# A decoder layer in float32 on one core: the last job keeps its split weights for both token tiles, the input's squares in two operations, no flush at the table load

## The chip, the core and the metric

The kernel runs on one core of one Trainium2 chip. The metric is the device time of the whole kernel in microseconds (us), as the median of several runs. TensorE multiplies matrices (PE in the profile; its weight loads are PEld), VectorE (DVE) and ScalarE (ACT) work elementwise, GpSimd (POOL) does little here, and SyncE (SP) issues DMAs from its queue in order.

## What is computed

One layer on 256 tokens of width 2048: a SwiGLU feed-forward network (FFN) at half weight, a mixer of attention and a short gated convolution, a second FFN, and a final normalisation.

```python
for l in range(DEPTH):                                  # DEPTH = 1
    x = x + 0.5 * swiglu(rms_norm(x, ffn1_norm[l]), ffn1_w_gate[l], ffn1_w_up[l], ffn1_w_down[l])
    x = x + hybrid_mixer(rms_norm(x, mix_norm[l]), w_in[l], b_gate[l], conv_w[l],
                         w_attn_out[l], w_conv_out[l], w_out[l])
    x = x + 0.5 * swiglu(rms_norm(x, ffn2_norm[l]), ffn2_w_gate[l], ffn2_w_up[l], ffn2_w_down[l])
return rms_norm(x, final_norm)

def swiglu(h, w_gate, w_up, w_down):                    # inner width 5632
    return (jax.nn.silu(h @ w_gate) * (h @ w_up)) @ w_down
```

## The kernel before

**Split weights.** All weights are float32 in HBM, 469 MB. For the products each is split into two parts of fewer bits: `hi` is the weight cast to fp32r, `lo` is the weight less `hi`. The activations are split in the same way and kept in SBUF. A product is then hi·hi + hi·lo + lo·hi, three matmuls.

**Chunks.** Weights come in chunks of 128x1024 (512 KB), one list of chunks for the whole kernel. `load` (L565) issues a chunk's DMA on SyncE's queue into one of five raw buffers `w`. `cut` (L572) makes `hi` on ACT (L578) and `lo` on DVE (L579), in one of four `hi` and four `lo` buffers. `parts` (L635) runs ahead of the chunk that TensorE is at (`done`): loads up to `done + 6`, cuts up to `done + 3`. A raw buffer is free when its chunk is cut, a `hi`/`lo` pair when TensorE has used it.

**Steps.** The program is a list `steps`, carried out in order of the list (L625); the order of instructions on every engine is the order in which they are written out. A step is a job on some chunks (`job`, `side_block`, `wide_job`, `v_step`) or a step without chunks. After a job, its closing work (`post`) goes to the list `pending`; `flush(1)` takes one entry of it behind each following chunk (L645). A step without chunks and with no `hold` empties the whole list first (L631). While `holding` is set, at the kernel's start, nothing is taken.

**Down projections.** An FFN runs in three rounds of its inner width (12, 16 and 16 of 44 slices). At the end of each round `wide_job` (L193) multiplies the round's slices, which lie in `ring`, with the down weights, for four column blocks (nb) of 512 columns. Here the activations are the stationary operand and the weights stream: for each chunk two slices x two token tiles x three matmuls. The mixer's output projection (L553) has the same form. `residual` (L224) closes a block: DVE adds the result to `x` (L231 or L233), ACT squares it for the next norm (`row_square`, L120), and, where another stage follows, four `turn` entries (L216) transpose four column slices of `x` on TensorE into the PSUM tiles `psT` and `psV` by turns and split them (L101, L102).

**The last round of the second FFN** has its own marks. `load_gain` (L260) brings 512 columns of the final gain on SyncE's queue into the single buffer `grow`, so it waits for the last multiply with the block before (L238). Block 3 is done as two `wide_job`s, one for each token tile (L349, L350), each with its own eight chunks; tile 0's closing work `finish` (L245: norm, scaling, output DMAs) runs while tile 1 is multiplied. In all three last rounds a step ahead of block 1 loads ScalarE's table for Sqrt (L346 and L555).

**The start.** The first FFN begins with `side_block` (L272): gate and up products of two slices in 16 half chunks (side chunks 0 to 15). Hooks at its chunks split the transposed input (`prepare`, L296), fetch the plain input (L583) and square its token tile 0 (`row_square_in`, L123: four operations of 512 columns on ACT, L128). The next job, ("g", 2), has chunks 16 and 17. Behind chunk 16 tile 1 is squared and `norm_cols` (L131: DVE, ACT's Sqrt, DVE) makes the norm; behind chunk 17 `rows` (L154) spreads it with matmuls on TensorE (L150), and `release` lets the closing work go.

Of the kernel before, what the change touches and what calls it, by code (L numbers as in the profile page):

```python
# [9 lines left out]
F32R = mybir.dt.float32r  # L10
AF = mybir.ActivationFunctionType
# [3 lines left out]
P = 128  # L15
D = 2048
T = 256
# [6 lines left out]
CW = CK * P  # L24
ROUNDS = ((0, 12), (12, 28), (28, 44))
NW = 4 * P
NB = D // NW
GK = 4
WARM = 6
RING = 17  # L30
LOAD_AHEAD = 6
SPLIT_AHEAD = 4
# [4 lines left out]
LINE = 32  # L37
# [13 lines left out]
def macaron_kernel(ctx: ExitStack, tc: tile.TileContext, xT, xt, gf, cst, wg1, wu1, wd1, win, wv, wao,  # L51
                   wco, wo, wg2, wu2, wd2, out):
    nc = tc.nc
# [3 lines left out]
    hpool = pool("hpool", 4)  # L57
    lpool = pool("lpool", 4)
# [15 lines left out]
    def ring(k):  # L74
        return phase["ring"][:, k, :]

    const.tile([P, 3 * LINE], F32, name="pad")
    x = const.tile([P, 2, D], F32, name="x")
    xn = const.tile([P, ND, 2 * T], F32R, name="xn")
    at = const.tile([P, ND, 2 * T], F32R, name="at")  # L80
# [24 lines left out]
    def psum_big(name):  # L105
        return pbig.tile([P, 2 * T], F32, name=name, tag="pbig")
# [7 lines left out]
    ssq = {}  # L114
# [8 lines left out]
    def row_square_in(i):  # L123

        if "f1" not in ssq:
            ssq["f1"] = work.tile([P, 2, NB], F32, name="ssq", tag="ssq", bufs=2)
        for nb in range(NB):
            nc.scalar.activation(at[:, i, :], x[:, i, nb * NW:(nb + 1) * NW], AF.Square,  # L128
                                 accum_out=ssq["f1"][:, i, nb:nb + 1])

    def norm_cols(tag, i0=0, i1=2):  # L131

        n = i1 - i0
        r = work.tile([P, 8], F32, name="rc", tag="rc", bufs=3)
        v, s, y = r[:, 0:n], r[:, 2:2 + n], r[:, 4:4 + n]
        nc.vector.reduce_sum(s, ssq[tag][:, i0:i1, :], axis=AX.X)
        nc.vector.tensor_scalar(v, s, 1.0 / D, EPS, op0=ALU.mult, op1=ALU.add)
        nc.scalar.activation(s, v, AF.Sqrt)
        nc.vector.reciprocal(y, s)
        nc.vector.tensor_mul(s, v, y)  # L140
        nc.vector.tensor_mul(s, s, y)
        nc.vector.tensor_scalar(s, s, -0.5, 1.5, op0=ALU.mult, op1=ALU.add)
        nc.vector.tensor_mul(r[:, 6:6 + n], y, s)
        rcol[tag] = r[:, 6:6 + n]
# [9 lines left out]
    def rows(tag):  # L154
        ps = norm_row(tag)
        R[tag] = work.tile([P, T], F32, name="R", tag="R", bufs=1)
        nc.vector.tensor_copy(R[tag], ps[:, 0:T])
# [32 lines left out]
    def wide(w, nb, k0=0, k1=ND):  # L190
        return [(w[nb][:, k * NW:(k + 2) * NW], CK) for k in range(k0, k1, 2)]

    def wide_job(chunks, src, post, tiles=(0, 1)):  # L193

        n = 2 * len(chunks)
        held = []

        def pe(parts):
            pv = {i: psum_big("pv") for i in tiles}
            held.append(pv)  # L200
            k = 0
            for hi, lo, _ in parts:
                for j in range(2):
                    cols = slice(j * NW, (j + 1) * NW)
                    a = src(k)
                    for i in tiles:
                        xh = a[:, i * P:(i + 1) * P]
                        xl = a[:, T + i * P:T + (i + 1) * P]
                        nc.tensor.matmul(pv[i], xh, hi[:, cols], start=(k == 0), stop=False)  # L209
                        nc.tensor.matmul(pv[i], xh, lo[:, cols], start=False, stop=False)  # L210
                        nc.tensor.matmul(pv[i], xl, hi[:, cols], start=False, stop=(k == n - 1))  # L211
                    k += 1
                yield
        return Step(chunks, pe, [lambda q=q: q(held[0]) for q in post], shift=0)

    def turn(m, gain):  # L216

# [46 lines left out]
    steps = []  # L264
# [35 lines left out]
    def ffn(tag, wg, wu, wd, gain_next, next_tag, first=False):  # L300
        gates = {}
        block = []

        def gu(t):
            def post_g(ps):
                g = merged(ps)
                nc.vector.tensor_mul(g, g, R[tag][:, 0:T])  # L307
                s = tmp("silu")
                nc.scalar.activation(s, g, AF.Silu)  # L309
                gates[t] = s  # L310

            def post_u(ps):
                u = merged(ps)
                nc.vector.tensor_mul(u, u, R[tag][:, 0:T])
                hh = tmp("hh")
                nc.vector.tensor_mul(hh, u, gates.pop(t))  # L316
                split_col(ring(t % RING), hh)

            rhs = lambda k: xn[:, k, :]
            for which, w, post in (("g", wg, post_g), ("u", wu, post_u)):  # L320
                if len(block) < (4 if first else 3):
                    block.append((w[t], post))
                    if first and len(block) == 4:
                        hooks = {n: [lambda k=n + 4: prepare(k, k + 4)] for n in (0, 4, 8)}
                        hooks[1] = [lambda: fetch(0)]
                        hooks[5] = [lambda: fetch(1)]
                        hooks[12] = [lambda: row_square_in(0)]
                        steps.append(Step([], lambda _: None, hold=True))
                        steps.append(side_block(block, rhs, hooks))
                    elif not first and len(block) == 3:  # L330
                        steps.append(side_block(block, rhs, seam_hooks(tag)))
                    continue
                late = {}
                if first and (which, t) == ("g", 2):
                    late = {0: lambda: (row_square_in(1), norm_cols(tag)), 1: lambda: (rows(tag), release())}
                steps.append(job((tag, which, t), pieces(w, t), rhs, post, late))

        t = 0
        for r, (k0, k1) in enumerate(ROUNDS):
            while t < min(k1 + 1, NF):  # L340
                gu(t)
                t += 1
            last = r == len(ROUNDS) - 1
            for nb in range(NB):
                if last and nb == 1:
                    steps.append(Step([], lambda _: nc.scalar.preload_act_table(AF.Sqrt)))  # L346
                if last and next_tag == "fin":
                    steps.append(Step([], lambda _, nb=nb: load_gain(nb), hold=False))
                split_last = last and next_tag == "fin" and nb == NB - 1  # L349
                for tiles in ((0,), (1,)) if split_last else ((0, 1),):  # L350
                    steps.append(wide_job(wide(wd, nb, k0, k1), lambda k, k0=k0: ring((k0 + k) % RING),
                                          residual(nb, 0.5, next_tag if last else None, gain_next), tiles))

    def mixer(gain_next, next_tag):
        rhs = lambda k: xn[:, k, :]
# [7 lines left out]
        held = {}  # L363
# [188 lines left out]

        for nb in range(NB):  # L553
            if nb == 1:
                steps.append(Step([], lambda _: nc.scalar.preload_act_table(AF.Sqrt)))  # L555
            steps.append(wide_job(wide(wo, nb), ring, residual(nb, None, next_tag, gain_next)))

    ffn("f1", wg1, wu1, wd1, GM, "mix", first=True)
    mixer(G2, "f2")
    ffn("f2", wg2, wu2, wd2, None, "fin")  # L560

    chunks = [c + (s.shift,) for s in steps for c in s.chunks]
    raw, split = [], []

    def load(n):  # L565
        while len(raw) < min(n, len(chunks)):
            src, nk, _ = chunks[len(raw)]
            w = wpool.tile([P, CW], F32, name="w", tag="w")
            nc.sync.dma_start(w[:, 0:nk * P], src)
            raw.append(w)  # L570

    def cut(n):  # L572
        while len(split) < min(n, len(chunks)):
            _, nk, off = chunks[len(split)]
            w = raw[len(split)][:, 0:nk * P]
            hi = hpool.tile([P, CW + 4 * LINE], F32R, name="hi", tag="hi")[:, off:off + nk * P]
            lo = lpool.tile([P, CW + 4 * LINE], F32R, name="lo", tag="lo")[:, off:off + nk * P]
            nc.scalar.copy(hi, w)  # L578
            nc.vector.tensor_sub(lo, w, f32(hi))  # L579
            split.append((hi, lo, nk))  # L580

    def fetch(i):
        nc.scalar.dma_start(x[:, i, :], xt[:, i, :])  # L583
# [32 lines left out]
    def release():  # L616
        nonlocal holding
        holding = False
# [6 lines left out]
    for s in steps:  # L625
        n = len(s.chunks)
        if s.hold is not None:
            holding = s.hold
        if not n:
            if s.hold is None:  # L630
                flush()  # L631
            s.pe(None)
            continue

        def parts(n=n):  # L635
            nonlocal done
            for _ in range(n):
                load(done + LOAD_AHEAD + 1)
                cut(done + SPLIT_AHEAD)
                yield split[done]  # L640
                done += 1

        gen = s.pe(parts())
        for _ in gen:
            flush(1)  # L645
        pending.extend(s.post if isinstance(s.post, list) else [s.post])
# [48 lines left out]
```

## Time and profile before

| | us |
|---|---|
| median of 3 runs | 2507.13 |
| lowest and highest | 2506.49, 2508.52 |
| the profiled execution | 2509.3 |
| its span, first to last instruction | 2507.5 |
| TensorE matmuls busy in the span | 2481.8 (99%) |
| VectorE busy | 1563.5 (62%) |
| ScalarE busy | 1183.8 (47%) |

The rows of the trace come from the one profiled execution; times in them are us from the start of its span. A matmul's row shows 0.39 us for 512 columns, but matmuls are pipelined, so their rate is read from start to start. TensorE's granted clock is shown as a share of full speed: 1.00 is 2.4 GHz and 0.50 is 1.2 GHz. Idle time of the other engines costs nothing as long as TensorE does not wait for it.

### The profile page before, as it was taken

Reading aid. Unit: us, or ns where it says so; the run is one execution under the profiler, and the core shown is the slowest. Engines: PE = TensorE matmul, PEld = TensorE weight load, DVE = VectorE, ACT = ScalarE, POOL = GpSimd, SP = SyncE. Lnnn points to the kernel's source line nnn. Section 1 sums busy time; section 2 is a strip of 40 time slices with the busy share of each in tenths; the row PEclk is TensorE's granted clock in tenths of the full one; section 3 lists DMA queues with packets and bytes.
Section 4 is the critical chain, followed back from the end, with each engine's and each line's share of the span. In section 5 each row is a group of like instructions: output and inputs, shape, how many; then the busy total and the mean of one; then the engine's idle time right before and its main releaser. Section 6 shows DMA issues by size and latency. Waiting matters only on the chain.

```text
span 2507.5 us, 34474 instructions
## 1 busy us (share of the span) xinstructions
PE 2481.8 (99%) x13384; PEld 2143.0 (85%) x13384; DVE 1563.5 (62%) x2135; ACT 1183.8 (47%) x1703; POOL 1.9 (0%) x10
## 2 busy tenths in 40 slices
PE   8999999999999999999999999999999999999997
PEld 7888888888888888888888888888888888888885
DVE  5665665566557777655566666665665566556655
ACT  6544444344445444444444454444544444444444
POOL 0000000000000000000000000000000000000000
PEclk9999999999999999999999999999999999999999
DMA  7565556655556555555555545565556555665565
GB/s 253 193 194 192 187 192 193 194 191 187 177 164 206 193 193 189 189 189 190 184 171 182 168 168 193 186 193 160 201 193 194 191 188 192 193 192 186 193 193 193
DMA packets 133651, 475.22 MB, mean 190 GB/s; under 512 B 14832, under 2 KB 14960, under 8 KB 133232
## 3 DMA queue, kind: packets, MB, share of 16 engines
q1 hardware_dynamic: 132480, 468.84, 58.1%
q10 hardware_dynamic: 1008, 4.19, 0.5%
q8 instruction: 104, 1.70, 0.3%
q14 instruction: 59, 0.48, 0.1%
HBM read 470.88 MB, written 2.10 MB: 189 GB/s over the span
## 4 chain that ended last, share of the span: by engine, by line
PE 97%; DMA 1%; DVE 1%; ACT 1%; issue 0%; SPq 0%; ACTq 0%
PE ps L169 45%; PE ps L170 23%; PE pv L211 7%; PE pv L210 7%; PE pv L209 7%; PE pv L449 1%; PE pv L447 1%; PE pv L448 1%; PE ps L284 1%; DMA w<-in_wu 1%; DMA w<-in_wd 1%; PE ps L285 1%; ACT hi L578 0%; DVE lo L579 0%; PE psV L504 0%; PE psS L470 0%
## 5 line engine op out<-in xcount | busy, mean ns | idle before, releaser
L579 DVE TENSOR_TENSOR lo<-w,hi 128x1024 fp32r<-128x1024 f32 (+1 forms) x908 | 1086.0, 1201 | 791.2 <-ACT hi L578 786.9
L169 PE MATMUL ps<-xn,hi 128*128 128x512 f32 x4448 | 1552.2, 393 | 1.2 <-DVE t L184 1.2
L170 PE MATMUL ps<-xn,lo 128*128 128x256 f32 x4448 | 1244.5, 280 | 0.0
L578 ACT CAST hi<-w 128x1024 fp32r<-128x1024 f32 (+1 forms) x908 | 928.0, 1028 | 660.8 <-PE pv L211 251.6
L169 PEld LDWEIGHTS ps<-xn,hi 128*128 128x128 f32 x4448 | 836.2, 188 | 185.4 <-issue 1.3
L170 PEld LDWEIGHTS ps<-xn,lo 128*128 128x128 f32 x4448 | 836.3, 188 | 1.0 <-DVE lo L579 0.3
L209 PE MATMUL pv<-hi,ring 128*128 128x512 f32 x832 | 327.4, 393 | 3.8 <-ACT hi L578 3.8
L210 PE MATMUL pv<-lo,ring 128*128 128x512 f32 x832 | 325.6, 391 | 3.0 <-DVE lo L579 3.0
L211 PE MATMUL pv<-hi,ring 128*128 128x512 f32 x832 | 325.0, 391 | 0.0
L209 PEld LDWEIGHTS pv<-hi,ring 128*128 128x128 f32 x832 | 156.9, 189 | 37.5 <-ACT hi L578 5.5
L210 PEld LDWEIGHTS pv<-lo,ring 128*128 128x128 f32 x832 | 157.2, 189 | 36.3 <-DVE lo L579 4.3
L211 PEld LDWEIGHTS pv<-hi,ring 128*128 128x128 f32 x832 | 157.1, 189 | 32.7
L184 DVE TENSOR_TENSOR t<-ps,c 128x256 f32<-128x256 f32 x320 | 133.6, 417 | 23.0 <-ACT c L182 23.0
L182 ACT COPY c<-ps 128x256 f32<-128x256 f32 x320 | 116.7, 365 | 54.4 <-PE ps L170 54.4
L98 ACT CAST ring<-hh 128x256 fp32r<-128x256 f32 x88 | 35.8, 406 | 201.2 <-DVE hh L316 201.2
L309 ACT ACTIVATE silu<-t 128x256 f32<-128x256 f32 x88 | 36.8, 418 | 163.3 <-DVE t L307 163.3
L169 PE MATMUL ps<-at,hi 128*128 128x512 f32 x256 | 89.5, 392 | 0.0
L169 PE MATMUL ps<-ring,hi 128*128 128x512 f32 x256 | 89.4, 392 | 0.0
L170 PE MATMUL ps<-ring,lo 128*128 128x256 f32 x256 | 71.6, 280 | 0.0
L170 PE MATMUL ps<-at,lo 128*128 128x256 f32 x256 | 71.6, 280 | 0.0
L99 DVE TENSOR_TENSOR ring<-hh,ring 128x256 fp32r<-128x256 f32 x88 | 37.4, 426 | 41.6 <-ACT ring L98 41.6
L284 PE MATMUL ps<-xn,hi 128*128 128x512 f32 x160 | 58.0, 401 | 0.7 <-ACT hi L578 0.7
(100 smaller groups left out, 1093.3 us busy)
## 6 DMA issues: line engine op xcount, KB each, us to landing
w<-in_win SPq DMA_DIRECT2D x218, 512.0 KB, 4.1
w<-in_wd SPq DMA_DIRECT2D x184, 512.0 KB, 3.9
w<-in_wu SPq DMA_DIRECT2D x170, 512.0 KB, 3.8
w<-in_wg SPq DMA_DIRECT2D x168, 512.0 KB, 3.6
w<-in_wco SPq DMA_DIRECT2D x32, 512.0 KB, 3.6
w<-in_wv SPq DMA_DIRECT2D x32, 512.0 KB, 4.3
w<-in_wao SPq DMA_DIRECT2D x32, 512.0 KB, 4.0
w<-in_wo SPq DMA_DIRECT2D x32, 512.0 KB, 4.1
```

Source lines behind the costliest of these rows:

```text
L99: nc.vector.tensor_sub(dst[:, T:2 * T], src, f32(dst[:, 0:T]))
L169: nc.tensor.matmul(ps, hi[:, j * P:(j + 1) * P], r, start=(k == 0), stop=False)
L170: nc.tensor.matmul(ps[:, 0:T], lo[:, j * P:(j + 1) * P], r[:, 0:T], start=False, stop=(k == n - 1))
L182: nc.scalar.copy(c, ps[:, T:2 * T])
L184: nc.vector.tensor_add(t, ps[:, 0:T], c)
L209: nc.tensor.matmul(pv[i], xh, hi[:, cols], start=(k == 0), stop=False)
L210: nc.tensor.matmul(pv[i], xh, lo[:, cols], start=False, stop=False)
L211: nc.tensor.matmul(pv[i], xl, hi[:, cols], start=False, stop=(k == n - 1))
L284: nc.tensor.matmul(ps[b], hi[:, j * P:(j + 1) * P], r, start=(k == 0), stop=False)
L309: nc.scalar.activation(s, g, AF.Silu)
L578: nc.scalar.copy(hi, w)
L579: nc.vector.tensor_sub(lo, w, f32(hi))
```

## The change

- The last job (block 3 of the second FFN's last round) becomes `last_job`: each chunk is loaded and cut once; TensorE goes through the eight chunks for token tile 0, keeps the split parts, and goes through them again for tile 1. Tile 0's closing work is written out behind the first chunk of the second pass. The split parts of the job's chunks 0 to 3 lie in `at` (the attention's output buffer, whose last use is in the mixer), those of chunks 4 to 7 in the pool buffers.
- `advance` takes the place of the two calls in `parts`. It counts only chunks in pool buffers against the four cut ahead, so chunks with a home are loaded and cut as soon as they are next in the list.
- The step that loads the Sqrt table has `hold=False`, so it no longer empties `pending`.
- `row_square_in` is one operation of 2048 columns for each token tile, with a memset of the sums on DVE; tile 0's moves from the hook at side chunk 12 to that at chunk 10, tile 1's from behind chunk 16 to the hook at chunk 15.

```diff
         if "f1" not in ssq:
             ssq["f1"] = work.tile([P, 2, NB], F32, name="ssq", tag="ssq", bufs=2)
-        for nb in range(NB):
-            nc.scalar.activation(at[:, i, :], x[:, i, nb * NW:(nb + 1) * NW], AF.Square,
-                                 accum_out=ssq["f1"][:, i, nb:nb + 1])
+            nc.vector.memset(ssq["f1"], 0.0)
+        junk = at[:, 4 * i:4 * i + 4, :].rearrange("p a b -> p (a b)")
+        nc.scalar.activation(junk, x[:, i, :], AF.Square, accum_out=ssq["f1"][:, i, 0:1])
...
+    def wide_tile(pv, i, a, hi, lo, cols, start, stop):
+        xh = a[:, i * P:(i + 1) * P]
+        xl = a[:, T + i * P:T + (i + 1) * P]
+        nc.tensor.matmul(pv, xh, hi[:, cols], start=start, stop=False)
+        nc.tensor.matmul(pv, xh, lo[:, cols], start=False, stop=False)
+        nc.tensor.matmul(pv, xl, hi[:, cols], start=False, stop=stop)
...
+    def last_job(chunks, src, post):
+        n = 2 * len(chunks)
+        kept = []
+        def tile_chunk(pv, i, c):
+            for j in range(2):
+                k = 2 * c + j
+                wide_tile(pv, i, src(k), *kept[c][0:2], slice(j * NW, (j + 1) * NW), k == 0, k == n - 1)
+        def pe(parts):
+            first, second = psum_big("pv"), psum_big("pv")
+            for c, part in enumerate(parts):
+                kept.append(part)
+                tile_chunk(first, 0, c)
+                yield
+            for c in range(len(chunks)):
+                tile_chunk(second, 1, c)
+                if c == 0:
+                    post[0]({0: first})
+                yield
+            held.append(second)
+        held = []
+        chunks = [c + (h if h < 4 else None,) for h, c in enumerate(chunks)]
+        return Step(chunks, pe, [lambda: post[0]({1: held[0]})], shift=0)
...
-                        hooks[12] = [lambda: row_square_in(0)]
+                        hooks[10] = [lambda: row_square_in(0)]
+                        hooks[15] = [lambda: row_square_in(1)]
...
-                    late = {0: lambda: (row_square_in(1), norm_cols(tag)), 1: lambda: (rows(tag), release())}
+                    late = {0: lambda: norm_cols(tag), 1: lambda: (rows(tag), release())}
...
-                    steps.append(Step([], lambda _: nc.scalar.preload_act_table(AF.Sqrt)))
+                    steps.append(Step([], lambda _: nc.scalar.preload_act_table(AF.Sqrt), hold=False))
...
-                split_last = last and next_tag == "fin" and nb == NB - 1
-                for tiles in ((0,), (1,)) if split_last else ((0, 1),):
-                    steps.append(wide_job(wide(wd, nb, k0, k1), lambda k, k0=k0: ring((k0 + k) % RING),
-                                          residual(nb, 0.5, next_tag if last else None, gain_next), tiles))
+                build = last_job if last and next_tag == "fin" and nb == NB - 1 else wide_job
+                steps.append(build(wide(wd, nb, k0, k1), lambda k, k0=k0: ring((k0 + k) % RING),
+                                   residual(nb, 0.5, next_tag if last else None, gain_next)))
...
     def cut(n):
         while len(split) < min(n, len(chunks)):
...
+            if home is None:
+                hi = hpool.tile([P, CW + 4 * LINE], F32R, name="hi", tag="hi")[:, off:off + nk * P]
+                lo = lpool.tile([P, CW + 4 * LINE], F32R, name="lo", tag="lo")[:, off:off + nk * P]
+            else:
+                hi, lo = (at[:, a:a + 2, :].rearrange("p a b -> p (a b)") for a in (2 * home, 8 + 2 * home))
...
+    def advance():
+        pooled = sum(c[3] is None for c in chunks[done:len(split)])
+        while len(split) < len(chunks):
+            if chunks[len(split)][3] is None:
+                if pooled == SPLIT_AHEAD:
+                    break
+                pooled += 1
+            load(len(split) + 1)
+            cut(len(split) + 1)
+        load(len(split) + LOAD_AHEAD + 1 - SPLIT_AHEAD)
...
-                load(done + LOAD_AHEAD + 1)
-                cut(done + SPLIT_AHEAD)
+                advance()
```

## Rows read from the trace of the kernel before

**Rows 1.** Timeline of PE, last job: start us, us, instruction.
```profile
2466.47 0.39 PE L209 MATMUL pv<-hi,ring 128*128 128x512 f32 x1
...
2471.68 0.39 PE L211 MATMUL pv<-hi,ring 128*128 128x512 f32 x1
...
2498.71 0.39 PE L211 MATMUL pv<-hi,ring 128*128 128x512 f32 x1
```

**Rows 2.** Windows: length, busy us and instructions of each engine, clock, DMA share, GB/s.
```profile
680.70:683.97 3.27, 1.62 (x9) 0.85 (x9) 1.86 (x4) 2.17 (x7) 0.00 (x0) 1.00 0.58 178
683.97:688.40 4.43, 4.43 (x14) 3.54 (x14) 2.16 (x3) 3.17 (x4) 0.00 (x0) 0.61 0.01 3
1688.57:1691.84 3.27, 1.61 (x9) 0.84 (x9) 1.86 (x4) 2.17 (x7) 0.00 (x0) 1.00 0.59 185
2444.90:2466.40 21.50, 21.50 (x96) 17.80 (x95) 12.30 (x12) 9.66 (x12) 0.00 (x0) 1.00 0.59 208
2471.91:2498.94 27.03, 20.15 (x73) 14.37 (x72) 17.91 (x23) 13.56 (x16) 0.00 (x0) 0.94 0.66 242
42.29:49.10 6.81, 5.66 (x17) 4.85 (x18) 4.26 (x9) 3.05 (x6) 0.00 (x0) 0.50 0.48 159
```

**Rows 3.** Waits of PE: who, for whom, total us, times, longest us.
```profile
PE psT L150 <- DVE rc L143: 2.6, 1, 2.6
...
PE ps L169 <- DVE t L184: 1.2, 1, 1.2
```

**Rows 4.** Groups by line and shape: count, busy us, mean ns, idle before.
```profile
L579 DVE TENSOR_TENSOR lo<-w,hi 128x1024 fp32r<-128x1024 f32 x868 | 1059.2, 1225 | 772.9 <-ACT hi L578 770.3 <-PE ps L285 0.6 <-PE ps L169 0.5
```

**Rows 5.** Timeline of SyncE's DMA queue, blocks 2 and 3 (xN: issues in a row).
```profile
2450.32 10.86 SPq L569 DMA_DIRECT2D w<-in_wd  x8
2471.66 0.33 SPq L262 DMA_DIRECT2D grow<-in_gf  x1
2472.08 10.87 SPq L569 DMA_DIRECT2D w<-in_wd  x9
```

**Rows 6.** Timeline of ACT and DVE in block 2, with the idle time before.
```profile
2454.83 1.05 ACT L578 CAST hi<-w 128x1024 fp32r<-128x1024 f32 x1 [3.03 <-DMA w<-in_wd]
2456.31 1.05 ACT L578 CAST hi<-w 128x1024 fp32r<-128x1024 f32 x1 [0.43 <-DMA w<-in_wd]
...
2466.67 1.05 ACT L578 CAST hi<-w 128x1024 fp32r<-128x1024 f32 x1 [1.67 <-PE pv L211]
...
2468.90 0.68 DVE L233 SCALAR_TENSOR_TENSOR x<-pv,x 128x512 f32<-128x512 f32 x1
```

**Rows 7.** Timeline of PE, first FFN's block 2: two turns, one chunk apart.
```profile
715.63 0.38 PE L221 MATMUL psT<-ident,x 128*128 128x128 f32 x2
...
718.62 0.38 PE L221 MATMUL psV<-ident,x 128*128 128x128 f32 x2
```

**Rows 8.** Timeline of the start, DVE, PE and ACT.
```profile
26.78 2.49 DVE L579 TENSOR_TENSOR lo<-w,hi 128x512 fp32r<-128x512 f32 x4
...
30.18 0.39 PE L284 MATMUL ps<-xn,hi 128*128 128x512 f32 x1
...
34.57 1.05 ACT L578 CAST hi<-w 128x1024 fp32r<-128x1024 f32 x1 [0.76 <-DMA w<-in_wu]
...
36.82 0.63 ACT L128 ACTIVATE at<-x 128x512 fp32r<-128x512 f32 x1
...
39.84 0.16 DVE L136 TENSOR_REDUCE rc<-ssq 128x2 f32<-128x8 f32 x1 [1.66 <-ACT at L128]
```

**Rows 9.** Groups of the page: count, busy us, mean ns.
```profile
L309 ACT ACTIVATE silu<-t 128x256 f32<-128x256 f32 x88 | 36.8, 418 | 163.3 <-DVE t L307 163.3
...
L169 PE MATMUL ps<-at,hi 128*128 128x512 f32 x256 | 89.5, 392 | 0.0
```

**Rows 10.** The instructions of line 346: duration in ns, first and last start.
```profile
L346 ACT ACT_TABLE_LOAD  x2: 1283/1283/1283, 684.8 to 2425.4; - x2
```

**Rows 11.** Timeline of ACT, first FFN: the squares of block 1.
```profile
710.61 0.60 ACT L120 ACTIVATE pv<-x 128x512 f32<-128x512 f32 x1 [1.89 <-DVE x L233]
```

More of the change, by code (lines that the diff above doesn't have):

```diff
@@ L191, in wide, with wide_job @@
         return [(w[nb][:, k * NW:(k + 2) * NW], CK) for k in range(k0, k1, 2)]
-    def wide_job(chunks, src, post, tiles=(0, 1)):
+    def wide_tile(pv, i, a, hi, lo, cols, start, stop):
[4 more added lines that the diff above has]
+        nc.tensor.matmul(pv, xl, hi[:, cols], start=False, stop=stop)
+    def wide_job(chunks, src, post):
         n = 2 * len(chunks)
@@ L198, in pe @@
         def pe(parts):
-            pv = {i: psum_big("pv") for i in tiles}
+            pv = {i: psum_big("pv") for i in range(2)}
             held.append(pv)
@@ L203, in pe @@
                 for j in range(2):
[L204 to L211, printed above, removed]
+                    for i in range(2):
+                        wide_tile(pv[i], i, src(k), hi, lo, slice(j * NW, (j + 1) * NW), k == 0, k == n - 1)
                     k += 1
@@ L554, in mixer @@
             if nb == 1:
-                steps.append(Step([], lambda _: nc.scalar.preload_act_table(AF.Sqrt)))
+                steps.append(Step([], lambda _: nc.scalar.preload_act_table(AF.Sqrt), hold=False))
             steps.append(wide_job(wide(wo, nb), ring, residual(nb, None, next_tag, gain_next)))
@@ L560, in macaron_kernel @@
     ffn("f2", wg2, wu2, wd2, None, "fin")
-    chunks = [c + (s.shift,) for s in steps for c in s.chunks]
+    chunks = [(c[0], c[1], s.shift, c[2] if len(c) > 2 else None) for s in steps for c in s.chunks]
     raw, split = [], []
@@ L566, in load @@
         while len(raw) < min(n, len(chunks)):
-            src, nk, _ = chunks[len(raw)]
+            src, nk = chunks[len(raw)][0:2]
             w = wpool.tile([P, CW], F32, name="w", tag="w")
@@ L573, in cut @@
         while len(split) < min(n, len(chunks)):
-            _, nk, off = chunks[len(split)]
+            _, nk, off, home = chunks[len(split)]
             w = raw[len(split)][:, 0:nk * P]
-            hi = hpool.tile([P, CW + 4 * LINE], F32R, name="hi", tag="hi")[:, off:off + nk * P]
-            lo = lpool.tile([P, CW + 4 * LINE], F32R, name="lo", tag="lo")[:, off:off + nk * P]
+            if home is None:
[3 more added lines that the diff above has]
+                hi, lo = (at[:, a:a + 2, :].rearrange("p a b -> p (a b)") for a in (2 * home, 8 + 2 * home))
             nc.scalar.copy(hi, w)
```

## The prediction, made before the changed kernel ran

> **What bounds the kernel now.** I read the windows first, then the waits of TensorE, then the timelines at the places they point to. TensorE sets the time: it is busy in nearly all of the span, and its 512-column matmuls follow each other in 0.2265 us (23 steps from 2466.47 to 2471.68 [rows 1]) whatever the other engines do. So only places where TensorE stands still, or runs at the lower of its two clock levels, can give anything back. There are four, and the change touches all of them.
>
> - *The last down-projection job.* From 2471.91 to 2498.94 us, 27.03 us, TensorE is busy for only 20.15 us, and that counts overlapped matmul tails [rows 2]. The job's first matmul starts at 2466.47, its last at 2498.71 [rows 1].
> - *The seam in the first FFN's last round*, between column block 0 and 1: 3.27 us from 680.70 with nothing but eight small transposes, then 4.43 us for a chunk at a mean granted clock of 0.61 [rows 2].
> - *The same seam in the mixer's output projection*: 3.27 us from 1688.57, no clock drop [rows 2].
> - *The start*: a wait of 2.6 us at L150 for the norm [rows 3], and right after it 6.81 us at a granted clock of 0.50 (1.2 GHz) [rows 2].
>
> **The last job, in before.** Why does it stall? It is done once per token tile, so each of the eight weight chunks is loaded, cast (ACT) and subtracted (DVE) twice, 16 chunks in all, and each feeds only six matmuls, 6 x 0.2265 = 1.36 us. A chunk costs DVE 1.225 us [rows 4], so DVE alone nearly fills that. Worse, the SyncE queue is in order and the gain load of block 3 (L262) waits in it for the last multiply with the old gain: it issues at 2471.66, and nine weight loads stand behind it from 2472.08 [rows 5]. TensorE has eaten the four chunks that were cut ahead by 2471.9 [rows 1] and starves.
>
> **The last job, after.** Eight chunks instead of sixteen are loaded and cut; the work of TensorE is the same 96 matmuls (8 chunks x 2 tiles x 6). Four chunks have a home in `at`, which nothing uses in this FFN, and take no pool buffer, so `advance` runs ahead: at block 2's chunk 4 it emits the cut of block 2's chunk 7 as before, then the cuts of chunks 0 to 3 of the last job, and the loads up to its chunk 6; one step later the load of chunk 7. All eight loads are now ahead of the gain load in SyncE's queue, so nobody stands behind it any more.
>
> Is each chunk there in time? In before, block 2's chunks 6 and 7 land at 2454.83 and 2456.31 (ACT waits for a DMA just until then) [rows 6], and eight loads go out in 10.86 us [rows 5], about 1.4 us each. ACT is in order: behind chunk 7's cut at 2456.31 come the five to eight new ones, at about 1.4 us each while loads limit them: chunk 0 near 2458, chunk 3 near 2463. Chunks 4 to 7 need a pool buffer that TensorE frees, the last when block 2 ends at 2466.63; that cut sits at 2466.67 in before as well [rows 6]. So chunk 7 is cut and subtracted by about 2470. TensorE wants chunk 0 at 2466.47 and chunk 7 at 2466.47 + 7 x 1.36 = 2476.0: margins of about 6 us on both. What is queued behind these cuts on ACT and DVE is only block 2's residual add, which ran from 2468.90 in before [rows 6] and has the same cut ahead of it. The second pass waits for nothing: all weights are kept. Tile 0's closing work (L233 to L256) lies beside the second pass.
>
> So 96 matmuls run without a gap: the last starts at 2466.47 + 95 x 0.2265 = 2487.99 instead of 2498.71 [rows 1], **-10.7 us**. Behind it comes the same chain of the last tile, 8.8 us to the end, unchanged. The half-clock stretch inside the old job lies within these 10.7 us and is not counted again.
>
> **The two seams.** The step that loads ScalarE's table emptied the list of pending work first. At the seam that is the residual add and four turns; TensorE's queue then holds eight transposes ahead of block 1's first chunk, and they wait for DVE's add, then in pairs for ACT and DVE to free two PSUM tiles. Without the flush, one entry follows each chunk of block 1, as at the later blocks. There a chunk with a turn takes 718.62 - 715.63 = 2.99 us against 12 x 0.2265 = 2.72 [rows 7], so a turn costs 0.27 us and four cost 1.08 us.
> - Mixer: 3.27 less 1.08: **-2.2 us** [rows 2].
> - First FFN: 3.27 + 4.43 - 2.72 - 1.08 = **-3.9 us**, of which 4.43 - 2.72 = 1.71 us is the clock alone [rows 2].
> - Second FFN: no turns there, so TensorE gains nothing; its gain load now stands ahead of the add in SyncE's queue and waits some 2 us longer, for which blocks 2 and 3 are the model: block 2's loads were held the same way until 2450.32 [rows 5], and TensorE was busy for all of 2444.90 to 2466.40 [rows 2]. 0.
>
> The table load itself (1.28 us) moves to ACT's idle time before the block's end. Its cover is ACT's wait for a weight buffer, 1.67 us between two cuts [rows 6]; uncovered it would put a cut back by at most 1.28 us, and the cuts stand three chunks, 8 us, ahead of TensorE.
>
> **The start.** Four squares of 512 columns become one of 2048. The one of 512 takes 0.63 us, and four with the reading of their sums last from 36.82 to 39.84, 3.0 us [rows 8]. The long one has no row. Its lower bound goes by the slope from 128x256 (0.418 us [rows 9]) to 128x512, 0.21 us per 256 columns: 0.63 + 6 x 0.21 = 1.9, and 0.15 for the sum; the upper one is the old 3.0. I take 2.1, as every ACT row here grows with its columns. That saves 0.9 us each on ACT. Tile 0's moves from side chunk 12 to 10; it also waits for a new memset on DVE, queued behind two subtractions that end near 26.78 + 2 x 0.62 = 28.0 [rows 8]. So ACT waits about 1 us, and with the 2.1 us square the cuts of side chunks 14 and 15 come some 3 us later: TensorE, which began chunk 14 at 30.18 [rows 8], waits about 1.3 us. That delay runs into the 2.6 us wait for the norm [rows 3] and vanishes in it.
>
> Does the norm come sooner? Tile 1's square moves from behind the cut of chunk 19 to ahead of it. But the norm's first operation is on DVE behind that same chunk's subtraction. Before: cut of chunk 18 ends 35.62, cut of 19, four squares, reduce at 39.84 [rows 8]. After: 35.62 + 2.1 (square) + 1.05 (cut) + 1.23 (subtraction) = 40.0. So the wait only changes its cause, **+0.2 us**, down to -0.6 if chunk 18, which waits for a DMA, lands earlier because fewer loads compete.
>
> The clock there is open. In before TensorE stands 2.6 us, works 0.7, stands 1.2 [rows 3] and then gets 1.2 GHz for 6.81 us, which costs 6.81 / 2 = 3.4 us [rows 2]. After, the first stand is about 1.6 us. From nothing gained to 3.4 us: I take 0, since most of the standing is still there, and keep both ends.
>
> The two seams show how loose this is: after the same 3.27 us stand the clock fell in one (mean 0.61 over the next chunk [rows 2]) and not in the other. The Trainium skill (TensorE: Matmul & The Clock Gate, Part 1) says that the gate's observation runs freely and does not restart with the kernel; the trace agrees, and by that rule the drop may be missing in other executions of before, and the one at the start may go.
>
> **The sum.** The profiled execution took 2509.3 us (its span is 2507.5): 2509.3 - 10.7 - 2.2 - 3.9 + 0.2 = 2492.7. It lies 2.2 us over the median of 2507.13, near the top of the runs; the 1.7 us of clock at the first seam is the likeliest difference. If the median run lacks it: 2507.1 - 10.7 - 2.2 - 2.2 + 0.2 = 2492.2. If it has it: 2490.5. With a little of the start's clock given back I say **2491.5**.
>
> **Rivals.**
> 1. *The start's low clock goes* (stand shortened to 1.6 us): 3.4 us more, 2487 to 2489. Against: 2.8 us of standing remain.
> 2. *The last job still starves.* If ACT's in-order cuts are held by a late load, TensorE waits in the first pass and a part of the 10.7 us stays; each us of landing beyond the 6 us margin costs one: 2494 to 2500. Against: the spacing of 1.4 us [rows 5].
> 3. *The squares force table loads.* Now block 0's squares follow the Sqrt table. If Square were not in that set, each place pays two loads of 1.28 us and the squares wait, and the turns with them; 3 x 2.6 = 7.7 us on ACT, of which at most 5 reach TensorE: 2496. Against: after the load at 684.8, which that line did twice in all [rows 10], squares run at 710.61 with nothing before them but the wait for the add [rows 11]. [...]
> 4. *Slower.* Half of the last job's matmuls (48) stream their weights from `at` instead of the pools. If `at` lies so that this streams slower, every one pays; 16.8 us of gain are used up when each takes 0.2265 + 16.8 / 48 = 0.58 us; at 0.70 the kernel ends near 2513. Against: matmuls that already stream from `at` take 392 ns by their records, as those from the pools do [rows 1, 9].
>
> **How the numbers follow.** Forecast (2489 to 2494) 0.65; rival 1 0.15; rival 2 0.12; rival 3 0.02; rival 4 0.02; a smaller gain for a reason not seen, near 2503, 0.04. Range 2487 to 2496: rival 1's lower end (2490.5 - 3.4), and 3.5 us over the sum for part of rival 2. A measurement of this kernel can tell about 0.2%, 5 us, from no change. Faster by more 0.94, within it 0.04, slower 0.02.
>
> **What would show it.** 176 weight loads of `wd` instead of 184; no TensorE gap between block 2's end and the last matmul, its 96 matmuls in about 21.8 us; no waits at L221; a wait at the norm's matmul still near 2 us with the norm ready near 41.5 us; no added table loads (11). Wrong if TensorE waits for casts in the last job, or if the seams keep a gap because the first turn still finds the add unfinished.

## The result, and the profile after

The changed kernel takes 2491.61 us (median of 4 runs, 2490.72 to 2492.07) against 2507.82 us for the kernel before beside it: ratio 0.9935, 95% interval 0.9918 to 0.9953. The forecast was 2491.5. The profiled execution took 2491.36 us with a span of 2489.6; the one of before took 2509.3 with a span of 2507.5, so this pair differs by 17.9 us.

To see where these went I took the start of each matmul of TensorE in both traces, in order, without the turns' transposes, and followed the difference from one to the next:

| stretch | forecast, us | measured, us |
|---|---|---|
| start, up to 76 us | +0.2 | -0.8 |
| seam of the first FFN, with the four turns behind it | -3.9 | -4.0 |
| seam of the mixer's output projection, with its turns | -2.2 | -2.4 |
| last job, first to last matmul (32.24 to 21.53) | -10.7 | -10.7 |
| last matmul to the end (8.81 in both) | 0 | 0 |

The waits of TensorE over the whole span come first (who, for whom, total us, times, longest us). Those of before at the turns (L221) and in the last job (L209, L210) have no successor here. The wait at the norm's matmul, 2.6 us in [rows 3], is 0.7; three of 3.4 us in all stand ahead of it, at the side chunks (L313), for ScalarE's casts, and most of that comes ahead of any instruction that the change touches.

```profile
PE ps L313 <- ACT hi L610: 3.4, 3, 1.8
PE ps L169 <- DVE t L184: 1.2, 1, 1.2
...
PE ps L170 <- DVE lo L611: 0.8, 1, 0.8
...
PE psT L150 <- DVE rc L143: 0.7, 1, 0.7
```

The windows (columns as in [rows 2]) of the last job and of the first FFN's seam: TensorE is busy in all of both, at full clock. The last row is a stretch at 1.2 GHz, near 18 us in this execution; the 6.8 us from 42.29 of [rows 2] are gone.

```profile
2459.23:2480.99 21.76, 21.76 (x97) 17.83 (x95) 10.30 (x19) 5.76 (x11) 0.00 (x0) 1.00 0.19 72
676.00:684.00 8.00, 8.00 (x37) 6.60 (x36) 4.61 (x5) 4.36 (x6) 0.00 (x0) 1.00 0.61 192
...
18.16:21.57 3.41, 3.41 (x10) 2.29 (x9) 2.40 (x6) 3.05 (x7) 0.00 (x0) 0.50 0.65 186
```

TensorE's timeline in the last job, first and last matmul, answers [rows 1]: 95 steps in 21.53 us, 0.2266 us each.

```profile
2459.23 0.39 PE L197 MATMUL pv<-at,ring 128*128 128x512 f32 x1
...
2480.76 0.39 PE L199 MATMUL pv<-hi,ring 128*128 128x512 f32 x1
```

SyncE's queue answers [rows 5]. The ten loads, two of block 2 and the job's eight, are all issued ahead of the gain load at 2466.11:

```profile
2443.08 13.05 SPq L598 DMA_DIRECT2D w<-in_wd  x10
2466.11 0.33 SPq L291 DMA_DIRECT2D grow<-in_gf  x1
```

ScalarE and VectorE answer [rows 6]. The casts into `at` and the four pool buffers follow each other about as the loads land. Chunk 0 is subtracted by 2453.05, where TensorE wants it at 2459.23; chunk 7, cast at 2461.11, by 2463.4, where it is wanted at 2468.75. So the margins were 6.2 and 5.3 us:

```profile
2450.73 1.05 ACT L610 CAST at<-w 128x1024 fp32r<-128x1024 f32 x1
...
2461.11 1.06 ACT L610 CAST hi<-w 128x1024 fp32r<-128x1024 f32 x1 [0.17 <-DMA w<-in_wd]
...
2451.82 1.23 DVE L611 TENSOR_TENSOR at<-w,at 128x1024 fp32r<-128x1024 f32 x1
...
2458.46 4.97 DVE L611 TENSOR_TENSOR lo<-w,hi 128x1024 fp32r<-128x1024 f32 x4 [1.47 <-ACT hi L610]
```

At the first FFN's seam the table load sits in ScalarE's idle time, and the turns stand one chunk apart, 2.98 us, as in [rows 7]; squares follow the load with no other load between them:

```profile
678.44 1.28 ACT L376 ACT_TABLE_LOAD   x1
680.09 1.05 ACT L610 CAST hi<-w 128x1024 fp32r<-128x1024 f32 x1 [0.36 <-PE pv L199]
683.03 0.60 ACT L120 ACTIVATE pv<-x 128x512 f32<-128x512 f32 x1 [1.89 <-DVE x L262]
...
688.05 0.38 PE L250 MATMUL psT<-ident,x 128*128 128x128 f32 x2
...
691.03 0.38 PE L250 MATMUL psV<-ident,x 128*128 128x128 f32 x2
```

The start answers [rows 8]. The square of 2048 columns takes 1.92 us, and 0.18 for its sum. ScalarE waits 0.92 us for the memset, and the norm's reduce runs right behind chunk 19's subtraction, at 40.44:

```profile
29.74 0.07 DVE L127 MEMSET ssq<- 128x8 f32 x1
...
29.85 1.92 ACT L129 ACTIVATE at<-x 128x2048 fp32r<-128x2048 f32 x1 [0.92 <-DVE ssq L127]
31.68 0.18 ACT L129 ACTIVATION_READ_ACCUMULATOR at<-x 128x1 f32 x1
...
39.29 1.23 DVE L611 TENSOR_TENSOR lo<-w,hi 128x1024 fp32r<-128x1024 f32 x1 [1.62 <-ACT hi L610]
40.44 0.15 DVE L136 TENSOR_REDUCE rc<-ssq 128x2 f32<-128x8 f32 x1
...
42.16 0.68 PE L150 MATMUL psT<-ident,rc 128*128 128x128 f32 x4 [0.65 <-DVE rc L143]
```

### The profile page after: what moved, and what is told of

It is laid out like the page before. It is cut to its first block, busy times and chain, and to the rows that moved or that the text cites. A ratio compares the mean times of both kernels' runs of the same rounds, so it can differ in the third digit from the quotient of the medians.

```text
span 2489.6 us, 34417 instructions
## 1 busy us (share of the span) xinstructions
PE 2473.3 (99%) x13384; PEld 2139.7 (86%) x13384; DVE 1554.7 (62%) x2128; ACT 1173.3 (47%) x1683; POOL 1.9 (0%) x10
## 4 chain that ended last, share of the span: by engine, by line
PE 97%; DVE 1%; DMA 1%; ACT 1%; issue 0%; ACTq 0%; SPq 0%
PE ps L169 45%; PE ps L170 23%; PE pv L199 8%; PE pv L197 8%; PE pv L198 8%; PE pv L478 1%; PE pv L477 1%; PE pv L476 1%; PE ps L313 1%; DVE lo L611 1%; ACT hi L610 1%; DMA w<-in_wg 1%; DMA w<-in_wu 0%; PE ps L314 0%; PE psV L533 0%; PE psS L499 0%
## 5 line engine op out<-in xcount | busy, mean ns | idle before, releaser
L611 DVE TENSOR_TENSOR lo<-w,hi 128x1024 fp32r<-128x1024 f32 (+1 forms) x896 | 1071.9, 1202 | 770.3 <-ACT hi L610 768.1
L610 ACT CAST hi<-w 128x1024 fp32r<-128x1024 f32 (+1 forms) x896 | 915.3, 1028 | 630.6 <-PE pv L199 224.9
L197 PE MATMUL pv<-hi,ring 128*128 128x512 f32 x816 | 319.6, 392 | 0.0
L199 PE MATMUL pv<-hi,ring 128*128 128x512 f32 x816 | 317.8, 390 | 0.0
L198 PE MATMUL pv<-lo,ring 128*128 128x512 f32 x816 | 317.8, 389 | 0.0
L199 PEld LDWEIGHTS pv<-hi,ring 128*128 128x128 f32 x816 | 153.2, 188 | 32.1
L197 PEld LDWEIGHTS pv<-hi,ring 128*128 128x128 f32 x816 | 153.2, 188 | 31.1
L313 PE MATMUL ps<-xn,hi 128*128 128x512 f32 x160 | 59.0, 407 | 3.4 <-ACT hi L610 3.4
```

The source lines that it names most:

```text
L197: nc.tensor.matmul(pv, xh, hi[:, cols], start=start, stop=False)
L198: nc.tensor.matmul(pv, xh, lo[:, cols], start=False, stop=False)
L199: nc.tensor.matmul(pv, xl, hi[:, cols], start=False, stop=stop)
L313: nc.tensor.matmul(ps[b], hi[:, j * P:(j + 1) * P], r, start=(k == 0), stop=False)
```

## The experiments

### One part of the change at a time

The last job alone: the changed kernel with the other two parts undone.

```diff
-                    steps.append(Step([], lambda _: nc.scalar.preload_act_table(AF.Sqrt), hold=False))
+                    steps.append(Step([], lambda _: nc.scalar.preload_act_table(AF.Sqrt)))
...
-                        hooks[10] = [lambda: row_square_in(0)]
-                        hooks[15] = [lambda: row_square_in(1)]
+                        hooks[12] = [lambda: row_square_in(0)]
```

> The kernel before with the last job alone changed (weights kept for both tiles, and the cutting ahead that goes with it); the table load still empties the list and the squares are as before. If the gain of the last job is TensorE's gaps there and nothing else, as predicted, the job's 96 matmuls take 21.5 us from first to last instead of 32.2, and the time falls by 10.7 us to about 2496.8 against a median of before near 2507.5. Rival: the job gains less by itself, because part of its gain rests on the earlier arrival of the loads after the other edits; then a gap stays in the job and the fall is under 9 us.

Measured: 2497.66 us against 2508.15 (median of the kernel before in this group of runs): -10.5 us, ratio 0.9959 (0.9945 to 0.9972). The job's matmuls take 21.53 us.

The flush alone: the kernel before with `hold=False` at both places.

```diff
-                    steps.append(Step([], lambda _: nc.scalar.preload_act_table(AF.Sqrt)))
+                    steps.append(Step([], lambda _: nc.scalar.preload_act_table(AF.Sqrt), hold=False))
```

> The kernel before with only the table load no longer emptying the list. If the seams are as predicted, each of the two seams with turns gives 2.2 us, and what the clock takes there (0 to 1.7 us each) on top: the time falls by 4.4 to 6.1 us, to about 2502. The block after the seam takes 2.99 us a chunk with a turn and there is no wait of TensorE at the transposes. Rival: the turns were paid anyway, by waits spread over the chunks; then the fall is under 2 us. The second FFN's seam gives 0 in both.

Measured: 2502.5 us against 2508.15: -5.65 us, ratio 0.9978 (0.9969 to 0.9987). At both seams 36 matmuls now take 8.16 us; in before the same 36, with the stand among them, took 13.17 and 11.55.

The squares alone: the kernel before with the new `row_square_in` and its new hooks.

> The kernel before with only the squares of the input in two operations, at the earlier places. Prediction: the wait at the norm's matmul shrinks but the norm itself is no earlier (0.2 us later), so the time stays within 1 us of before, less up to 3.4 us where TensorE's low clock after the wait is missing. Rival that the trace of the changed kernel suggests: what is gained by the clock is taken back, because from the norm to about 72 us cutting and closing work on ScalarE and VectorE take 3.7 us a chunk where TensorE takes 2.8; then at most 1 us is left at 75 us, whatever the clock did.

Measured: 2508.08 us against 2508.15, ratio 1.0002 (0.9993 to 1.0011).

The changed kernel without the squares:

> The changed kernel with the squares put back (four operations each, at the old places). If the parts add, the time is before less 10.7 less 4.4 to 6.1, thus about 2491.5 against a median of before near 2507.5, and within 1 us of the changed kernel. If the squares were worth 1 to 3 us by the clock, it is 2493 to 2494.

Measured: 2492.4 us, ratio 0.9938 (0.9925 to 0.9950). The single parts add up to 10.5 + 5.65 + 0.07 = 16.2 us, the whole to 16.2 in its first runs and 17.3 in these:

> The changed kernel itself beside the others, on the same chip: about 2491.6 by the first runs; by the sum of the single edits measured so far (10.5 for the last job, 5.65 for the flush, 0.1 for the squares) 16.2 under the kernel before.

Measured: 2491.12 us against 2508.39, ratio 0.9934 (0.9922 to 0.9947).

### Why the last job stalled in before

The prediction put the stall on the doubled cutting and, "worse", on the gain load in SyncE's queue. With a second gain buffer the gain load waits for nobody:

```diff
-        grow[nb] = work.tile([P, NW], F32, name="grow", tag="grow", bufs=1)
+        grow[nb] = work.tile([P, NW], F32, name="grow", tag="grow", bufs=2)
```

> The kernel before with two buffers for the final gain instead of one, so the gain load no longer waits in SyncE's queue for the block before; the last job still loads and cuts its weights twice. If the queue was the larger part of the last job's stall, TensorE no longer starves at 2472 to 2478 and the job's 96 matmuls take some 25 us instead of 32.2: 6 to 7 us faster. Rival: the stall is the doubled cutting itself (1.225 us on VectorE for 1.36 us of matmuls, with tile 0's closing work of about 5 us in the same queues) and the doubled loads; then the weights come no sooner and the fall is under 3 us.

Measured: 2507.47 us against 2508.39, ratio 0.9999 (0.9990 to 1.0008). In its trace the job's matmuls take 30.2 us instead of 32.2. Counting the sixteen chunks of both tiles from 0, TensorE in before waits at chunk 4 (from 2471.7, 1.3 us in its two waits), at chunk 6 (from 2476.3, 1.7), at chunk 12 (from 2488.3, 2.5) and at chunk 15 (from 2495.5, 1.3). The last of these came by SyncE's queue: tile 0's output DMAs (L256) stand in it ahead of the job's last weight load. TensorE's rows at chunks 12 and 15, and SyncE's:

```profile
2490.47 0.50 PE L209 MATMUL pv<-hi,ring 128*128 128x512 f32 x1 [1.78 <-ACT hi L578]
...
2496.42 0.49 PE L209 MATMUL pv<-hi,ring 128*128 128x512 f32 x1 [0.55 <-ACT hi L578]
```
```profile
2489.30 1.31 SPq L256 DMA_DIRECT2D out_y<-sacc  x3
2490.66 0.69 SPq L569 DMA_DIRECT2D w<-in_wd  x1
```

With two gain buffers the wait at chunk 4 is the same, those at chunks 6 and 15 are gone, and the one at chunk 12 has grown to 4.1 us, as TensorE's timeline (only rows with a wait) shows. ScalarE's rows show what chunk 12 waits for: three casts of tile 1 stand behind the scaling of tile 0's output (L255) and start right as it ends.

```profile
2470.13 0.50 PE L209 MATMUL pv<-hi,ring 128*128 128x512 f32 x1 [0.58 <-ACT hi L578]
2471.39 0.50 PE L210 MATMUL pv<-lo,ring 128*128 128x512 f32 x1 [0.76 <-DVE lo L579]
2486.15 0.50 PE L209 MATMUL pv<-hi,ring 128*128 128x512 f32 x1 [3.32 <-ACT hi L578]
2487.41 0.80 PE L210 MATMUL pv<-lo,ring 128*128 128x512 f32 x1 [0.76 <-DVE lo L579]
```
```profile
2484.34 0.83 ACT L255 ACTIVATE sacc<-sacc,rc 128x640 f32<-128x640 f32 x1 [1.00 <-DVE rc L143]
2485.07 2.92 ACT L578 CAST hi<-w 128x1024 fp32r<-128x1024 f32 x3
```

So tile 0's closing work, which I had left out of the account of before, was the next suspect. I wrote it out at the end of the kernel instead, first with two gain buffers:

```diff
+                if split_last:
+                    steps[-1].post = steps[-2].post + steps[-1].post
+                    steps[-2].post = []
```

> The kernel before with two buffers for the gain and with tile 0's closing work written out at the very end, ahead of tile 1's, instead of among tile 1's cuts. What is measured is the time from the first to the last of the last job's 96 matmuls, which was 32.2 us in before, 30.2 with two gain buffers alone and 21.5 with kept weights; the tail behind it gets about 5 us longer. If tile 0's closing work in the queues of ScalarE and VectorE makes the rest of the stall, the matmuls take under 27 us. If the doubled cutting does (16 subtractions of 1.225 us are 19.6 us on VectorE, behind the closing of block 2 and behind loads at 1.3 us), they stay over 28 us.

Measured: 2501.79 us against 2508.59, ratio 0.9975 (0.9963 to 0.9986), though the tail behind the last matmul grew from 8.8 to 10.9 us. The job's matmuls take 24.15 us; these waits are left, 1.5 us:

```profile
2470.64 0.50 PE L209 MATMUL pv<-hi,ring 128*128 128x512 f32 x1 [0.58 <-ACT hi L581]
2471.90 0.50 PE L210 MATMUL pv<-lo,ring 128*128 128x512 f32 x1 [0.76 <-DVE lo L582]
2481.91 0.50 PE L210 MATMUL pv<-lo,ring 128*128 128x512 f32 x1 [0.19 <-DVE lo L582]
```

And the same with the single gain buffer:

> The kernel before with tile 0's closing work at the very end, as in the run before this one, but with the single gain buffer again. That run's matmuls took 24.15 us with two gain buffers. If the gain load in SyncE's queue costs only the 2 us that it cost beside the closing work (32.2 against 30.2), they take about 26 us here. If it was covered by the closing work and shows its price only without it, they take 28 us or more.

Measured: 2506.0 us against 2507.94, ratio 0.9991 (0.9981 to 1.0000); the job takes 27.6 us. The four give a square:

| first to last matmul of the last job, us | closing work among tile 1's cuts | at the end |
|---|---|---|
| one gain buffer | 32.2 (before) | 27.6 |
| two gain buffers | 30.2 | 24.15 |

With the weights kept it is 21.5. Before the cells are compared, the clock has to be: 3.4 us of the job run at 1.2 GHz in three of the four, at one of the waits, and none with two gain buffers and late closing work. TensorE's rows with one buffer and late closing work show it behind the wait at chunk 6: matmuls start 0.43 us apart instead of 0.2265.

```profile
2477.64 0.50 PE L209 MATMUL pv<-hi,ring 128*128 128x512 f32 x1 [1.43 <-ACT hi L581]
...
2479.92 0.63 PE L209 MATMUL pv<-hi,ring 128*128 128x512 f32 x1
2480.35 0.63 PE L210 MATMUL pv<-lo,ring 128*128 128x512 f32 x1
```

By the starts of these slow matmuls the low clock adds 1.4 us to the 27.6 and 1.5 to the 30.2; this is an estimate, and it takes no wait elsewhere into account. With that taken out, the gain load costs 32.2 - 30.2 = 2.0 us beside the closing work and 27.6 - 1.4 - 24.15 = 2.1 without it; the closing work costs 32.2 - 27.6 = 4.6 us beside the gain load and 30.2 - 1.5 - 24.15 = 4.6 without it. So of the 10.7 us tile 0's closing work holds 4.6, the gain load 2.0, the low clock behind their waits 1.5, and 2.6 are left. Each cell is one trace; in two more with the old job (the flush alone, the squares alone) it took 32.8 and 32.4, so tenths of a us count for little.

Most of the 2.6 us is the stand at chunk 4, 1.9 us by the starts and the same in all four. Four chunks cut ahead last 24 x 0.2265 = 5.4 us in a job that does each chunk for one tile only, and the fifth cast stands on ScalarE behind the squares of block 2, closing work as well. How the 1.9 us divides between the two is not shown. ScalarE's rows with two buffers and late closing work:

```profile
2468.93 0.60 ACT L120 ACTIVATE pv<-x 128x512 f32<-128x512 f32 x1 [0.60 <-DVE x L233]
...
2469.56 4.86 ACT L581 CAST hi<-w 128x1024 fp32r<-128x1024 f32 x5
```

### Is it the early loads or the kept weights?

The changed kernel with homes for chunks 0 to 3, but with those counted among the four cut ahead:

```diff
-        pooled = sum(c[3] is None for c in chunks[done:len(split)])
+        ahead = len(split) - done
         while len(split) < len(chunks):
-            if chunks[len(split)][3] is None:
-                if pooled == SPLIT_AHEAD:
-                    break
-                pooled += 1
+            if ahead == SPLIT_AHEAD:
+                break
+            ahead += 1
```

> The changed kernel with the last job's chunks 0 to 3 still in their homes, but counted among the four that are cut ahead, so loads go no further ahead than before: those of chunks 6 and 7 stand behind the gain load in SyncE's queue again. If that wait is what the early loads avoid, TensorE waits for chunk 6, whose load goes out near the time at which block 3's first chunk has run for 5.6 us and lands 4 us later: a gap of 2 to 5 us, the time between the changed kernel's and that much more, 2494 to 2497. Rival: keeping the weights is all that matters, since only eight chunks are cut at 2.7 us of matmuls each; then the time is the changed kernel's within 1 us.

Measured: 2492.15 us beside 2491.12 for the changed kernel. Two loads do stand behind the gain load again, but TensorE waits only 0.68 us for them, and the job takes 22.5 us, 1.0 more. Of SyncE's and TensorE's timelines:

```profile
2461.33 0.33 SPq L291 DMA_DIRECT2D grow<-in_gf  x1
2461.75 0.86 SPq L598 DMA_DIRECT2D w<-in_wd  x2
```
```profile
2468.27 0.50 PE L198 MATMUL pv<-lo,ring 128*128 128x512 f32 x1 [0.68 <-DVE lo L611]
```

So it is the kept weights that bring nearly all of it; cutting further ahead brings 1.0 us of the job in the traces, less than the times can tell.

### The start

The norm's reduce stands behind chunk 19's subtraction on VectorE. Moved ahead of it, with the memset at the kernel's beginning and tile 0's square back behind side chunk 12:

```diff
-                        hooks[10] = [lambda: row_square_in(0)]
-                        hooks[15] = [lambda: row_square_in(1)]
+                        hooks[12] = [lambda: row_square_in(0)]
+                        hooks[15] = [lambda: (row_square_in(1), norm_cols(tag))]
...
```

> The changed kernel with three moves at the start: the memset of the sums stands at the kernel's beginning, tile 0's square back behind side chunk 12, and the norm's operations right behind tile 1's square, ahead of chunk 19's cut. If the wait for the norm was due to VectorE's queue (the reduce stood behind chunk 19's subtraction), the norm is ready 2 us earlier, TensorE does not wait at the norm's matmul, and the backlog of closing work starts 2 us earlier: 1 to 2.5 us faster than the changed kernel. Rival: the start is bound by the loads until side chunk 18; then within 0.5 us of the changed kernel.

Measured: 2490.33 us beside 2491.12, ratios to before 0.9932 (0.9919 to 0.9944) and 0.9934: the times can't tell them apart. In the trace the norm's last operation starts at 39.04 instead of 41.86, TensorE no longer waits at the norm's matmul, and the last matmul comes 1.2 and 1.0 us earlier than in the two traces of the changed kernel. VectorE's rows:

```profile
37.61 0.16 DVE L133 TENSOR_REDUCE rc<-ssq 128x2 f32<-128x8 f32 x1 [0.30 <-ACT at L126]
...
39.04 0.16 DVE L140 TENSOR_TENSOR rc<-rc 128x2 f32<-128x2 f32 x1
```

Its median is the lowest of this study, by 0.8 us, which is no more than the noise.

## Why the prediction was right, and where not

**The sum.** Its three large terms were right to 0.2 us in the traces, and the median fell in the middle of the range. That it came within 0.1 us of the forecast is luck: the median of before beside it lay 0.7 us above the one that the sum began with, and the start gave 0.8 us where 0.2 was to be lost. The last job's term did not depend on why the old job was slow: it was the old span less 96 steps of 0.2265 us, and the margins that it needed (about 6 us forecast, 6.2 and 5.3 measured) were there.

**The account of the old last job was wrong.** "Worse, the SyncE queue" made the gain load the main culprit; freeing it brought nothing that the time can show (0.9999, with an interval that reaches to 2.5 us), and putting two loads behind it again in the changed kernel cost 0.68 us of wait. By the traces it held 2.0 of the 10.7 us. What the account lacked was closing work in the in-order queues. Tile 0's, among tile 1's cuts on ScalarE and VectorE and ahead of the last weight load on SyncE, held 4.6 us, and the low clock behind the waits 1.5; block 2's squares stood ahead of the cast at which TensorE first waited. I had mentioned tile 0's only for the changed kernel, where it lies beside the second pass because no cut stands behind it any more.

**The seams** went as worked out. Without a drop of the clock a seam costs 3.4 us of stand, of which the turns take 1.08 back. How much the clock adds could not be read from one trace: in the six traces here that still have the flush, that is twelve passes of a seam, four are followed by 3.4 us at 1.2 GHz (the first FFN's at 684.0 in before and at 683.0 in the second run with late closing work; the mixer's near 1689 in the last job alone and in the squares alone), always behind the same stand. A third of 1.7 us at each of two seams is 1.1 us, and 2.3 + 2.3 + 1.1 = 5.7 fits what the flush alone gave (5.65), though its interval, 3.3 to 7.8 us, would hold 4.6 without any drop too. The assumption that the median of before held less low clock than the profiled execution is borne out by the mean granted clock on record for each run. It was 0.996 in the profiled execution; of the 59 runs of before beside the experiments 18 had 0.996 (median 2509.05 us), 22 had 0.997 (2508.6) and 19 had 0.998 (2506.45). Whether the seam is the place where the others lack it is not on record. The Trainium skill (TensorE: Matmul & The Clock Gate, Part 1) says that the gate's observation runs freely; the twelve passes agree.

**The start** was small, as forecast, but two steps were wrong. The norm was expected near 41.5 us with a wait for it of 1.6 us in the working and near 2 us among the signs; it was ready near 42.0 and TensorE waited 0.7, because TensorE itself came later. TensorE's timeline at the side chunks:

```profile
6.92 0.51 PE L313 MATMUL ps<-xn,hi 128*128 128x512 f32 x1 [1.26 <-ACT hi L610]
...
16.64 0.51 PE L313 MATMUL ps<-xn,hi 128*128 128x512 f32 x1 [1.76 <-ACT hi L610]
...
32.42 0.50 PE L313 MATMUL ps<-xn,hi 128*128 128x512 f32 x1 [0.35 <-ACT hi L610]
```

The first two waits, 3.0 us, are for loads that land late, ahead of the first new square, and differ from trace to trace: 0.4, 1.0 and 0.7 us in the second trace of the changed kernel, 1.6 and 0.3 with the flush alone. Only the third, 0.35 us, stands behind the memset and the earlier square, which were priced at 1.3; it is 0.35 in the second trace too, and 1.46 in that of the squares alone. And rival 1 came true without its price. The low clock behind the norm is missing in all five traces with squares at side chunks 10 and 15 or 12 and 15 (the changed kernel twice, the squares alone, four cut ahead, the early norm), while five of the seven others have it, before for 6.8 us and four for 3.4; two of the five have 3.4 us of it earlier instead, near 18 us (changed kernel) and 30 us (squares alone). But the 3.4 us, which is the price of the 6.8 us in before's trace alone, don't arrive. In the trace of the changed kernel TensorE was 2.0 us ahead of before at 49 us and 0.8 at 76 us. It is the same without the new squares: at 76 us the two traces with the old ones and no low clock there (the flush alone, late closing work with two buffers) are 0.6 and 0.4 us ahead of before, and the four with 3.4 us of it lie between 0.3 us behind and 0.9 ahead. ScalarE's timeline shows where it went:

```profile
59.51 1.03 ACT L610 CAST hi<-w 128x1024 fp32r<-128x1024 f32 x1
...
63.09 0.41 ACT L98 CAST ring<-hh 128x256 fp32r<-128x256 f32 x1 [2.28 <-DVE hh L345]
63.41 1.05 ACT L610 CAST hi<-w 128x1024 fp32r<-128x1024 f32 x1
...
66.60 0.42 ACT L338 ACTIVATE silu<-t 128x256 f32<-128x256 f32 x1 [1.88 <-DVE t L336]
66.92 1.03 ACT L610 CAST hi<-w 128x1024 fp32r<-128x1024 f32 x1
```

Casts follow each other at 3.9 and 3.5 us, 7.4 us for two chunks, while TensorE needs 2.77 us a chunk. ScalarE waits for VectorE in each entry of the held-back closing work, one per chunk, with a cast and a subtraction in between. TensorE lives on the four chunks cut ahead until they are used up: at 71.92 it starts a chunk whose `lo` comes late and waits 0.77 us. A TensorE that starts this stretch earlier loses a part of its lead there: 1.2 us in each of the seven traces without the low clock behind the norm, none in the five with it. So rival 1's price was mis-sized: the squares alone gave 0.07 us, and the changed kernel with and without them differs by about 1 us, within the noise. In the trace of the early norm, where the closing work begins earlier too, TensorE is 2.5 us ahead of before at 76 us, 1.4 more than in the second trace of the changed kernel; the times do not show it.

**Rival 2** (the last job still starves) did not come: no wait of TensorE in it, and 176 weight loads of `wd` instead of 184. **Rival 3** neither: eleven table loads in both kernels, and squares 3.3 us behind the moved load without another. The Trainium skill (ScalarE: Activation LUTs, section on table sets) does not name Square among the fillers of every set, and leaves open what else the Sqrt set holds. Here Square runs under the Sqrt table (683.03, above) as well as under Silu's (in before at 681.1 us, ahead of the Sqrt load at 684.8), with no load between. **Rival 4** neither; two groups of the changed kernel's page, weights from `at` and from the pools:

```profile
L197 PE MATMUL pv<-hi,ring 128*128 128x512 f32 x816 | 319.6, 392 | 0.0
...
L197 PE MATMUL pv<-at,ring 128*128 128x512 f32 x16 | 6.2, 389 | 0.0
```

## What to carry to other kernels

A stall's size can be forecast from the bounding engine's own spacing (old stretch less the number of its instructions times their step) even while its cause is misread; but the cause decides what else would help, so move each suspected piece of work away by itself before calling it the cause. Where small closing work is written out among the preparations of the next piece, in-order queues make the next piece wait for it: look in the queue ahead of the operation that the bounding engine waits for. And a gain ahead of a stretch that another engine limits is in part only lent, so look for the next such stretch before counting it.

## What the runs showed that I had not expected

- The same stand of TensorE at a seam (3.3 us with eight small transposes) was followed by 1.2 GHz in 4 of 12 passes, for 3.4 us each time, at 1.7 us of cost: two profiles of one kernel can differ by that without any change in the program.
- One trace of each version can mislead. The gain load seemed to cost 2.0 us beside the closing work and 3.4 without it; the difference, 1.4 us, is a stretch at 1.2 GHz that one trace of the second pair has and the other has not. Five of the six traces with the old last job have such a stretch in it, and none of the six with kept weights.
